# Output projection of a hybrid encoder block: eight pairs of token tiles with seven part products, placed in the up/down stream, in place of sixteen single tiles

## The chip, the cores and the metric

One core of one Trainium2 chip runs the whole program. The time is the device time of one execution in microseconds. The kernel before took 2931.34 us, the median of three runs (2931.17 to 2938.84).

## The reference, cut to what matters

The block has 2048 tokens of 1024 columns. An input projection feeds two groups of heads, a chunked mLSTM (y_A, 512 columns) and latent attention (y_B, 512 columns). Then:

```python
h = h + jnp.concatenate([y_a, y_b], axis=-1) @ w_out[l]          # 1024 x 1024
h = h + conv_gated_mlp(rms_norm(h, ln_ffn_g[l]), w_up[l], ...)   # d_ff 2816, 2 x 2816 columns up
gate = jax.nn.sigmoid(rms_norm(h, ple_norm_g[l]) @ w_ple_gate[l])
h = h + gate * rms_norm(p[l] @ w_ple_proj[l], ple_post_g[l])
out = rms_norm(h, final_g)
```

The change concerns the first of these lines and the normalisation that opens the second.

## The kernel before

Every matrix product is made to the accuracy of fp32 from three products of high and low parts: `split` (L108) writes a copy rounded to fp32r on ACT (L119) and the rest by a subtraction on DVE (L122), and `mm3` (L129) issues low x high, high x low and high x high (L132). A token tile is 128 tokens; there are 16.

`run` (L149) calls the stages in order: the input projection, `attend`, `out_proj`, `up_down`. Each has its own tiles in SBUF, named by tags ("w5", "x10", "u1", "t0"); a new tile on a tag waits until the last reader of the old one is done. PSUM has eight banks: while attention and output projection run, four of them are "sc" (`bank`), two "tr" (`tbank`), one "pv" and one "ml". After `out_proj` these pools are closed and others are opened for the up stage, two of [x, y] and two of [z, spare].

**Attention** (`attend`, L1193) runs 64 rounds, one for each of 4 heads x 16 token tiles. The order of a round is written out by hand (L1232): score banks of the next tile ("s0" to "s3"), their exponentials ("E", "e"), transposes ("t"), the product with the values ("V"), and a dot for each place at which the mLSTM, which runs beside it as a generator, may take a step. `SIDE` (617) sets how many steps are spread over the 64 rounds; what is left of it is done after the last round. The row sums of the softmax are collected, inverted, transposed and stored to `ri_d` in two halves (`sums`, L1244), through a tile "ri" on the tag u1.

**Output projection** (`out_proj`, L1349). The 1024 rows of the weights are eight k-tiles. Their splits stay in SBUF ("wo"); those of the mLSTM half are scaled by that group's gain. `load_y(c)` (L1327) loads the turned columns of a token tile ("yr") and the reciprocal row sums, spread over all partitions ("rb", through `row_bcast`, L145), multiplies the attention half by them (L1332) and splits ("yhl"). Then come, for both column halves, 8 k-tiles x 3 products into a bank, and DVE adds the bank to the tile of x (L1383). The rows go to `h1_d` (L1384), for the residual later. `norm_load` (L1297) squares and sums the row on ACT, makes the inverse root on POOL, and scales the row by it and by the gain g2 in place with one operation of DVE (L1303), which must wait for the store to `h1_d`. One tile later eight transposes of TensorE turn it (L1312), ACT copies the two banks (L1313), and the turned tile goes to `x2_d`. In between lie loads of the convolution taps and the operands of the first block of the up stage: `sums(0)` reads four 128x512 pieces of `x2_d` back at a time, makes four sums on DVE, splits three of the operands (B11, T1, T2) and stores the other two to `t_d`.

**Up and down stage** (`up_down`, L1649). It goes by blocks and, within a block, by pairs. A pair is a product of a 2 x 2 array of parts A (stationary operand, split by `up_prep`) with a 2 x 2 array B (moving operand, 512 columns, split by `load_op` or `sum4`), made with seven part products in place of eight:

```
T1 = B12 - B11   T2 = B22 - T1   T3 = T2 - B11   T4 = B21 - T2
S1 = A21 + A22   S2 = S1 - A11   S3 = A11 - A21  S4 = A12 - S2
A11 B11,  S1 T1,  S2 T2,  A12 B21,  S3 T3,  A22 T4,  S4 B22
```

Each part product is 4 k-tiles x 3 products of 512 columns (`prod`, L507; the products at L512). A22 T4 and S4 B22 of a pair are issued in the middle of the next one (`rest_y`, L1664; `rest_z`, L1679), and with them what is added to them. The loop (`for i in range(n)`) has seven places at which other work is let in (`side(1)` to `side(7)`), and at a block's end the operands of the next are loaded there. Pairs 0 and 1 are written a little differently from the others, since the operands of block 0 are only then complete.

Of the kernel before, what the change touches and what calls it, by code (L numbers as in the profile page):

```python
# [37 lines left out]
SIDE = 617  # L38
# [22 lines left out]
class Block:  # L61
# [4 lines left out]
    def __init__(self, ctx, tc, d):  # L66
# [31 lines left out]
        self.t_d = dt([2, 4, P, 4, 512], F32, name="t_d")  # L98
        self.tw_d = dt([4, 4, P, 4, 512], F32, name="tw_d")
# [49 lines left out]
    def run(self, out):  # L149
# [9 lines left out]
        self.attend(tail(self.mlstm()))  # L159
        self.out_proj()  # L160
        right.close()
        pools(right, "right", ("fa", 2))
        left.close()
        pools(left, "left", ("fb", 2))
        self.up_down(out)
# [16 lines left out]
    def in_proj(self):  # L182
# [158 lines left out]
        cols = self.cst.tile([P, 8], F32, name="cols")  # L341
# [851 lines left out]
    def attend(self, side):  # L1193
# [50 lines left out]
        def sums(half):  # L1244

            pt = self.tbank([NH * 8, P])
            nc.tensor.transpose(pt, rsums[:, half * NH * 8:(half + 1) * NH * 8], self.ident)
# [4 lines left out]
        cur, self.wo = self.first, []  # L1252
        pts, pend = [], None
        for i, (h, qt) in enumerate(seq):
            if h == NH - 1 and qt in (4, 6, 8, 10):
                self.load_wo(qt // 2 - 2)
            if h == NH - 1 and qt == 9:
                sums(0)
            if i == len(seq) - 2:
                self.y0 = self.load_y(0)  # L1260
# [5 lines left out]
            if nxt is None:  # L1266
                self.ps0 = self.pml.tile([P, 512], F32, name="wo0", tag="ml")
                self.out_mm(self.ps0, self.y0, range(4), slice(0, 512))
            for op in order:
                if op == ".":  # L1270
                    pump()
                elif op[0] == "s" and nxt:
                    score_bank(nxt, int(op[1]))
                elif op[0] == "t":
# [15 lines left out]
            cur = nxt  # L1290
        pv(pend, 1)
        sums(1)
        for _ in side:
            pass


    def norm_load(self, h, g, ssq_junk):  # L1297

        nc = self.nc
        ssq = self.stat(1, "nt_s")  # L1300
        nc.scalar.activation(ssq_junk, h, AF.Square, accum_out=ssq)
        r = self.rsq(ssq, 1, 1.0 / D)
        nc.vector.scalar_tensor_tensor(h, h, r, g, op0=ALU.mult, op1=ALU.mult)  # L1303

    def transpose_out(self, xn, otag, dst):
        nc = self.nc
        pt = (self.tbank(), self.tbank())
        xo = self.at(otag, [P, KT, P], name="nt_o")
        for f in range(2):
            for j in range(4):  # L1310
                kt = f * 4 + j
                nc.tensor.transpose(pt[f][:, j, :], xn[:, kt * P:(kt + 1) * P], self.ident)  # L1312
            nc.scalar.copy(xo[:, f * 4:f * 4 + 4], pt[f])  # L1313
        nc.sync.dma_start(dst, xo)

    def load_wo(self, k):
        nc = self.nc
        raw = self.at(("w13", "w13", "w13", "w13", "w13", "w12", "u2", "w0")[k], [P, D], name="wor")
        nc.sync.dma_start(raw, self.d["w_out"][0, k * P:(k + 1) * P, :] if k < 4 else self.wo_d[k - 4])
        w = self.at(f"x{(0, 1, 2, 3, 6, 7, 4, 5)[k]}", [P, 2, D], F32R, f"wo{k}")  # L1320
        if k < NH:
            self.split_g(raw, self.gmix[:, k:k + 1], w[:, 0], w[:, 1])
        else:
            self.split(raw, w[:, 0], w[:, 1])
        self.wo.append(w)

    def load_y(self, c):  # L1327
        yr = self.at(f"w{5 + c % 2}", [P, 8, P], name="yr")
        self.nc.sync.dma_start(yr, self.y_d[c])
# [83 lines left out]

# [754 lines left out]
```

## Time and profile before

| | |
|---|---|
| median of three runs | 2931.34 us |
| the profiled execution | 2930.37 us, span 2928.6 us, mean granted clock 0.994 |
| input projection and start (0 to 200 us) | PE busy 182.59 us |
| attention (200 to 1160) | PE busy 948.84, DVE 721.19, ACT 548.61 |
| end of attention (1160 to 1228) | PE busy 60.44 of 68.00 |
| output projection and first operands (1228 to 1420) | PE busy 188.55 of 192.00, DVE 97.13, ACT 63.70 |
| up stage (1420 to 2160) | PE busy 737.31 of 740.00 |
| down stage, gate and end (2160 to 2930) | PE busy 742.80 of 770.00 |

The profile comes from one execution. Times are microseconds; a group's row has its busy time, the mean of one instruction in ns, and the idle time of the engine just before it with what ended that. PE is TensorE, DVE VectorE, ACT ScalarE, POOL GpSimd, and SP issues nearly all DMAs, in one queue. A timeline's row has start, busy time, engine, line, operation, and in brackets the wait before it and what ended the wait.

### The profile page before, as it was taken

How to read it: one execution, taken by the hardware profiler on the slowest of the kernel's cores; microseconds unless marked ns; L12 is line 12 of the kernel's file. 1: busy time of each engine (PE TensorE's matmuls, PEld its weight loads, DVE VectorE, ACT ScalarE, POOL GpSimd, SP SyncE). 2: the span in 40 equal slices, each digit the busy share in tenths (PEclk: the TensorE clock that was granted, in tenths of full speed). 3: DMA queues.
4: the chain of work that ended last, by engine and by line, in shares of the span. 5: the costliest groups of instructions: out<-in, count | busy, mean ns of one | idle time of the engine just before them, and what ended most of it. 6: DMA issues, size and time to landing. Idle time of an engine off the chain costs nothing.

```text
span 2928.6 us, 40726 instructions
## 1 busy us (share of the span) xinstructions
PE 2860.5 (98%) x14543; PEld 2405.6 (82%) x14543; DVE 2098.0 (72%) x3727; ACT 1525.7 (52%) x2919; POOL 152.6 (5%) x295
## 2 busy tenths in 40 slices
PE   8899999999999999899999999999999999999998
PEld 7788888988988898788788887888887788888776
DVE  7566878767777777535777777777778766676776
ACT  7544556555666665423555555655556333244664
POOL 4100000000000000000000000000000000002011
PEclk9999999999999999999999999999999999999999
DMA  9766655443333343468635544657776657575864
GB/s 276 219 197 183 185 169 167 136 128 96 96 101 106 105 128 104 140 202 282 207 132 189 178 170 158 193 181 236 233 237 201 225 200 230 179 245 202 284 190 151
DMA packets 424954, 530.19 MB, mean 181 GB/s; under 512 B 31504, under 2 KB 286512, under 8 KB 424752
## 3 DMA queue, kind: packets, MB, share of 16 engines
q1 hardware_dynamic: 424752, 527.60, 56.2%
q8 instruction: 114, 1.87, 0.3%
q14 instruction: 88, 0.72, 0.1%
HBM read 347.49 MB, written 180.02 MB: 180 GB/s over the span
## 4 chain that ended last, share of the span: by engine, by line
PE 78%; DVE 7%; DMA 6%; ACT 4%; issue 3%; POOL 1%; SPq 0%; POOLq 0%; ACTq 0%; DVEq 0%
PE fxy L512 30%; PE fz L512 12%; PE bk L132 7%; PE ppv L132 5%; PE bk L512 4%; PE tb L1209 3%; PE tb L512 2%; PE bk L1146 2%; PE bk L1148 2%; PE bk L1150 2%; PE bk L1147 2%; PE bk L1149 2%; PE fs L132 1%; PE mb L1085 1%; PE mb L1086 1%
## 5 line engine op out<-in xcount | busy, mean ns | idle before, releaser
L512 PE MATMUL fxy<-op,fw 128*128 128x512 f32 x3552 | 856.1, 393 | 15.9 <-DVE fh L1653 4.6
L512 PEld LDWEIGHTS fxy<-op,fw 128*128 128x128 f32 x3552 | 662.0, 188 | 174.2 <-ACT ug L1817 12.9
L512 PE MATMUL fz<-op,fw 128*128 128x512 f32 x1776 | 441.2, 391 | 5.4 <-DVE xt L1383 2.6
L512 PEld LDWEIGHTS fz<-op,fw 128*128 128x128 f32 x1776 | 332.8, 188 | 74.9 <-DVE xt L1383 2.8
L119 ACT CAST pt<-tb 128x512 fp32r<-128x512 f32 x256 | 147.3, 586 | 188.1 <-PE tb L1209 187.3
L512 PE MATMUL fxy<-op,fwd 128*128 128x512 f32 (+1 forms) x888 | 214.0, 389 | 1.0 <-ACT gate L2001 0.8
L1151 DVE TENSOR_REDUCE mx<-bk 128x1 f32<-128x512 f32 x255 | 174.7, 685 | 47.0 <-PE bk L1150 46.4
L132 PE MATMUL ppv<-pt,kv 128*128 128x256 f32 x1536 | 204.9, 288 | 0.0
L122 DVE TENSOR_TENSOR pt<-tb,pt 128x512 fp32r<-128x512 f32 x256 | 174.4, 686 | 31.0 <-ACT pt L119 29.9
L512 PEld LDWEIGHTS fxy<-op,fwd 128*128 128x128 f32 x888 | 165.1, 188 | 36.0 <-ACT gate L2001 1.2
L132 PEld LDWEIGHTS ppv<-pt,kv 128*128 128x128 f32 x1536 | 190.1, 192 | 0.3 <-ACT pt L119 0.3
L1169 ACT ACTIVATE pe<-bk,nm 128x512 f32<-128x512 f32 x255 | 173.8, 696 | 27.4 <-DVE nm L1163 26.3
L132 PE MATMUL bk<-wo,yhl 128*128 128x512 f32 x744 | 176.4, 395 | 5.8 <-DVE yhl L122 5.8
L132 PEld LDWEIGHTS bk<-wo,yhl 128*128 128x128 f32 x744 | 139.5, 190 | 34.8 <-DVE yhl L122 6.2
L132 PE MATMUL bk<-wsp,xh 128*128 128x464 f32 (+1 forms) x512 | 156.5, 387 | 0.0
L1209 PE MATMUL tb<-ident,pe 128*128 128x128 f32 x1024 | 149.8, 273 | 4.0 <-DVE pt L122 3.6
L1209 PEld LDWEIGHTS tb<-ident,pe 128*128 128x128 f32 x1024 | 121.6, 140 | 23.1 <-DVE pt L122 7.0
L119 ACT CAST fw<-hraw 128x1024 fp32r<-128x1024 f32 (+1 forms) x72 | 70.2, 981 | 125.2 <-PE fxy L512 96.0
L1653 DVE TENSOR_TENSOR fh<-fh,fxy 128x512 f32<-128x512 f32 x95 | 65.1, 686 | 91.8 <-PE fxy L512 91.3
L122 DVE TENSOR_TENSOR fw<-fwr,fw 128x1024 fp32r<-128x1024 f32 x88 | 107.5, 1221 | 29.2 <-ACT fw L119 29.2
L1704 DVE SCALAR_TENSOR_TENSOR fgv<-uv,fcw,fgv 128x1024 f32<-128x1024 f32 x88 | 112.8, 1282 | 10.6 <-ACT fgv L1702 9.9
L1146 PE MATMUL bk<-kv,q_s 128*128 128x512 f32 x255 | 114.4, 449 | 1.0 <-ACT pe L1169 1.0
(431 smaller groups left out, 5025.8 us busy)
## 6 DMA issues: line engine op xcount, KB each, us to landing
fwr<-in_w_up SPq DMA_DIRECT2D x66, 512.0 KB, 4.7
fh<-h_d SPq DMA_DIRECT2D x48, 512.0 KB, 3.7
h_d<-fh SPq DMA_DIRECT2D x48, 512.0 KB, 4.5
s_d<-fwr SPq DMA_DIRECT2D x44, 512.0 KB, 2.6
fws<-s_d SPq DMA_DIRECT2D x44, 512.0 KB, 3.9
rw<-row_d SPq DMA_DIRECT2D x32, 512.0 KB, 5.0
tw_d<-tsum SPq DMA_DIRECT2D x60, 256.0 KB, 5.4
opr<-tw_d SPq DMA_DIRECT2D x60, 256.0 KB, 4.6
```

What stands on the lines that cost most here:

```text
L119: nc.scalar.copy(hi, src)
L122: (sub or nc.vector).tensor_tensor(lo, src, _f(hi), op=ALU.subtract)
L132: mm = lambda *a, **k: self.nc.tensor.matmul(*a, **k, skip_group_check=more)
L512: self.nc.tensor.matmul(out, a[:, k * P:(k + 1) * P], parts[lo][:, cols], start=first, stop=lo == 1 and k == last, skip_group_check=more)
L1146: mm(ps, ql, kh[:, ks], start=True, stop=False)
L1147: mm(ps, qr, self.krl[:, ks], start=False, stop=False)
L1148: mm(ps, qh, kl[:, ks], start=False, stop=False)
L1151: nc.vector.tensor_reduce(s.mx[:, kb:kb + 1], ps, axis=AX.X, op=ALU.max)
L1169: nc.scalar.activation(s.pe[:, kb % 2], s.banks[kb], AF.Exp, bias=s.nm, scale=ASCALE, accum_out=s.rs[:, kb:kb + 1])
L1209: nc.tensor.transpose(t[:, j, :], s.p[kb][:, j * P:(j + 1) * P], self.ident)
L1653: add = lambda o, a, b: tt(o, a, b, op=ALU.add)
L1704: nc.vector.scalar_tensor_tensor(t, u[:, tap:tap + 2 * SB], taps[:, tap, ct:ct + 1], t, op0=ALU.mult, op1=ALU.add)
```

## The change

**The projection becomes eight pairs.** `out_proj`, `load_wo`, `load_y`, `out_mm`, `norm_load` and `transpose_out` are gone. `up_down` becomes a generator `stream`, whose loop starts at pair -8. In pairs -8 to -1, A is two token tiles (rows) by two halves of the 1024 columns of y, and B is `w_out` as 2 x 2 parts of 512 x 512. Pairs -8 to -5 hold the tiles c and c + 4 (c = 0 to 3), pairs -4 to -1 the tiles 8, 9 to 14, 15.

**The operands of the weights.** `out_sums` makes T1 to T4 of the weights in rounds 33 to 60 of attention and stores them to `two_d`; the splits of B11 and T1 follow there. T2, B21 and T3 are loaded and split in the last rounds, T4 and B22 right after the last.

**The end of attention.** The mLSTM's steps are spread with `SIDE` 660 and all done four rounds before the end. The first pair's tiles are loaded then. In the last round, which has no scores, the generator issues A11 B11 and S1 T1 of pair -8 at "s0" and "s2". "ri" lies on the tag s2 in place of u1.

**The rows.** The norm is in `norm`: squares in two halves on ACT, the sum and the inverse root on POOL, and the scaling in place by ACT, behind the store to `h1_d`. The gain g2 is applied later: `turn` makes four transposes into a bank and four scaled copies of 128 columns each on ACT. The first row of a pair is turned two pairs later at places 2 and 3 (`old`), the second one pair later at 6 and 7 (`prev`).

**Sums of block 0 on chip.** `sums4` makes T1 to T4 of block 0 from the turned tiles c and c + 4 while they are in SBUF and stores them to `t_d`. The turned tile of the half B12 is not stored in these pairs. Block 0 is then loaded like every other block, while pair -1 runs, and pairs 0 and 1 are written like the others. PSUM keeps the pools of attention to the end: x and y from "sc", z from "tr", the spare bank from "pv" and "ml" in turn. The places of the split operands in SBUF (OPX, PAIRS) are dealt anew.

The diff, cut to its core:

```diff
-SIDE = 617
+SIDE = 660
-        self.attend(tail(self.mlstm()))
-        self.out_proj()
...
-        self.up_down(out)
+        self.attend(tail(self.mlstm()), self.stream(out))
...
-            o = self.at("u1", [NH * 8, P], name="ri")
+            o = self.at("s2", [NH * 8, P], name="ri")
...
+        last = {"s0": lambda: next(stream), "s2": lambda: next(stream), "s3": lambda: self.op_split("T3")}
+            if 33 <= i < 61:
+                next(wout, None)
+            if i == n - 4:
+                for _ in side:
+                    pass
+                self.up_load(-8)
+                self.op_load("T2", ("t0", "t1", "t2", "t3"))
+            if i == n - 3:
+                later = self.up_prep(-8)
+            if i == n - 2:
+                self.op_load("B21", ("t4", "t5", "u0"))
+            if i == n - 1:
+                self.op_split("T2")
+                later()
+                self.op_load("T3", ("u1", "t0", "t1"))
+                self.op_split("B21")
...
+        self.op_load("T4", ("t2", "t3", "t4", "t5"))
+        self.up_load(-7)
         pv(pend, 1)
         sums(1)
+        self.op_split("T4")
+        self.op_load("B22", ("t0", "t1", "t2", "t3"))
+        self.op_split("B22")
...
+        for e, tag in enumerate(("w12", "w13", "w0", "w1")[i % 2 * 2:i % 2 * 2 + 2]):
+            c = self.out_tile(i, e)
+            t = self.at(tag, [P, 8, P], name="yr")
+            self.nc.sync.dma_start(t, self.y_d[c])
+            raw[i].append((t, self.row_bcast(self.at(f"t{6 + e}", [P, SB], name="rb"), self.ri_d[c].rearrange("h t -> (h t)"), SB)))
...
+        def norm(s, e):
+            h, ssq, half = s.o[e], self.stat(2, "nts"), self.stat(1, "nt_s")
+            nc.sync.dma_start(self.h1_d[self.out_tile(s.i, e)], h)
+            for f, fs in enumerate((L, H)):
+                nc.scalar.activation(self.at("s2", [P, SB], BF16, "junk"), h[:, fs], AF.Square, accum_out=ssq[:, f:f + 1])
+            nc.gpsimd.tensor_tensor(half, ssq[:, 0:1], ssq[:, 1:2], op=ALU.add)
+            r = self.rsq(half, 1, 1.0 / D)
+            nc.scalar.activation(h, h, AF.Copy, scale=r)
+        def turn(s, e, f, bank):
+            pt = bank.rearrange("p (k t) -> p k t", t=P)
+            for j in range(4):
+                nc.tensor.transpose(pt[:, j, :], s.o[e][:, (f * 4 + j) * P:(f * 4 + j + 1) * P], self.ident)
+            xo = self.at(f"t{f if s.i < -4 and not e else 4 + f}", [P, 4, P], name="nt_o")
+            for j in range(4):
+                nc.scalar.activation(xo[:, j], pt[:, j], AF.Copy, scale=self.g2[:, f * 4 + j:f * 4 + j + 1])
...
+        def begin(at):
+            bank = prev.spare if at % 2 and prev and prev.spare is not None else s.spare
+            if at in (6, 7) and prev and prev.out:
+                turn(prev, 1, at - 6, bank)
+            if at in (2, 3) and old and old.out:
+                turn(old, 0, at - 2, bank)
+            if at in (3, 4, 5) and old and old.i < -4:
+                sums4(old, at)
...
-        for i in range(n):
+        for i in range(-8, n):
```

In the order of TensorE, the end of attention before. The last products of the first token tile are mixed with the last transposes of the mLSTM (mb<-ident,hy); "wo" numbered 12186 to 13287 are k-tiles of the weights, and the first row with wo_11630 opens token tile 1.

```order
L1113 MATMUL mb<-ident,hy 128x128 x4
L132 MATMUL bk<-wo_12186,yhl 128x512
L132 MATMUL bk<-wo_12478,yhl 128x512 x3
L132 MATMUL bk<-wo_13272,yhl 128x512 x3
L132 MATMUL bk<-wo_13277,yhl 128x512 x3
L132 MATMUL bk<-wo_13282,yhl 128x512 x3
L132 MATMUL bk<-wo_13287,yhl 128x512 x3
L132 MATMUL bk<-wo_11630,yhl 128x512 x3
L132 MATMUL bk<-wo_11889,yhl 128x512 x3
```

The same place after: behind the last products with the values (ppv) and the transpose of the row sums (tb<-ident,gt). fw_13270 and 13271 hold S2 and S4 of pair -8, fw_13043 and 13044 its A11 and A12, fw_13052 its S3 and S1; fw_13485 is A11 of pair -7.

```order
L133 MATMUL ppv<-pt,kv_4664 128x256 x2
L1242 MATMUL tb<-ident,gt 32x128
L507 MATMUL bk<-op,fw_13270 128x512 x3
L507 MATMUL bk<-op,fw_13271 128x512 x4
L507 MATMUL bk<-op,fw_13270 128x512 x4
L507 MATMUL bk<-op,fw_13043 128x512 x4
L507 MATMUL bk<-op,fw_13044 128x512 x4
L507 MATMUL bk<-op,fw_13043 128x512 x4
L507 MATMUL bk<-op,fw_13485 128x512 x3
L507 MATMUL bk<-op,fw_13052 128x512 x4
```

The mLSTM's transposes have moved ahead of this place, and between the last product with the values and the first operand of pair -7 stand 23 products of pair -8.

In SP's queue, the same place before: the last store of attention's output (y_d<-ya), the second half of the row sums (ri_d<-ri), the weights of the first up pair (fwr), then the loads of token tile 1.

```order
L1227 DMA y_d<-ya 128x128 x2
L1250 DMA ri_d<-ri 32x128
L1562 DMA fwr<-in_w_up 128x8x128
L1329 DMA yr<-y_d 128x1024
L1115 DMA y_d<-hy 128x512
L146 DMA rb<-ri_d 128x512
L1354 DMA xt<-in_x 128x1024
L1384 DMA h_d<-xt 128x1024
L146 DMA rb<-ri_d 128x512 x2
```

After: opw are pieces of the output weights (here B22), yr and rb the tiles and row sums of the pairs.

```order
L1575 DMA xt<-in_x 128x1024
L1566 DMA yr<-y_d 128x1024 x3
L1362 DMA opw<-wo_d 128x512 x4
L1222 DMA y_d<-ya 128x128 x2
L1245 DMA ri_d<-ri 32x128
L147 DMA rb<-ri_d 128x512 x2
L1575 DMA xt<-in_x 128x1024
```

The loads of the tiles and of B22 now stand ahead of the last store of attention's output, and no store of the mLSTM stands between them and their row sums.

On ACT in the projection, before, while the operands of block 0 are made: casts of the token tiles (yhl) and of block 0's operands (op<-tsum), the squares (junk), the copies of the turned tile (nt_o).

```order
L119 CAST yhl<-yr 128x1024
L119 CAST op<-tsum 128x512
L1313 COPY nt_o<-tb 128x512 x2
L1301 ACTIVATE junk,nt_s<-xt 128x1024
L119 CAST op<-tsum 128x512 x3
```

After, in pair -4: the squares of both rows in halves (L1697), the scaling (L1700), the casts of the next pair's operands (fw), and the scaled copies of 128 columns (L1710).

```order
L1697 ACTIVATE junk,nts<-xt 128x512
L1710 ACTIVATE nt_o<-fs,cols 128x128
L1697 ACTIVATE junk,nts<-xt 128x512 x2
L1700 ACTIVATE xt<-xt,rsr 128x1024
L120 CAST fw_14246<-yr 128x1024
L120 CAST fw_14240<-yr 128x1024
L1710 ACTIVATE nt_o<-fs,cols 128x128
L1697 ACTIVATE junk,nts<-xt 128x512
L1710 ACTIVATE nt_o<-fs,cols 128x128 x3
L120 CAST fw_14434<-yr 128x1024
L1710 ACTIVATE nt_o<-fs,cols 128x128 x4
L1700 ACTIVATE xt<-xt,rsr 128x1024
```

The scaling of the whole row, and 16 small copies for each pair, are new on ACT; the next pair's casts stand behind the scaling.

More of the change, by code (lines that the diff above doesn't have):

```diff
@@ L1273, in attend @@
                     score_bank(nxt, int(op[1]))
+                elif op in last and not nxt:
+                    last[op]()
                 elif op[0] == "t":
@@ L1316, in load_wo @@
[L1316 to L1325, printed above, removed]
```

366 lines of the change are left out of this document (182 added, 184 removed).

## The prediction

> **What bounds the kernel now.** I read the page first, then the stretches of time with the busy time of each engine, then TensorE's timeline around the stage that is changed, and last the chain of waits there.
>
> ```profile
> span 2928.6 us, 40726 instructions
> PE 2860.5 (98%) x14543; PEld 2405.6 (82%) x14543; DVE 2098.0 (72%) x3727; ACT 1525.7 (52%) x2919; POOL 152.6 (5%) x295
> ```
>
> TensorE is busy for 98% of the span, and no other engine is near that. A microsecond is won only by giving TensorE fewer products or by closing one of its few gaps. The next rows show where the gaps of the changed stretch are (the columns are the length of the stretch, busy us of PE, its weight loads, DVE, ACT and POOL, the granted clock, the DMA share and GB/s).
>
> ```profile
> 1220.00:1240.00 20.00, 14.20 (x54) 11.26 (x54) 5.97 (x7) 2.19 (x3) 0.77 (x2) 0.83 0.58 180
> 1246.00:1340.00 94.00, 94.00 (x447) 77.56 (x446) 37.62 (x49) 24.60 (x41) 5.10 (x14) 1.00 0.61 205
> 1340.00:1380.00 40.00, 39.84 (x188) 33.01 (x187) 28.46 (x41) 16.34 (x28) 2.94 (x8) 1.00 0.93 306
> 1400.00:1420.00 20.00, 17.43 (x75) 13.95 (x73) 13.34 (x18) 11.87 (x23) 1.69 (x4) 0.91 0.94 294
> 1420.00:1790.00 370.00, 370.00 (x1630) 303.51 (x1630) 282.66 (x350) 193.48 (x269) 0.00 (x0) 1.00 0.48 165
> ```
>
> Inside the output projection (1246 to 1380) TensorE has no gap, and DVE and ACT are at 40% and 26%. The gaps are at its two ends. The up stage that follows runs 370 us without a gap, with DVE at 76%. TensorE's timeline gives the ends and the pace:
>
> ```profile
> 1205.49 0.51 PE L132 MATMUL wo<-wo,yhl 128*128 128x512 f32 x1 [0.70 <-ACT wo L119]
> 1208.52 5.76 PE L132 MATMUL ppv<-pt,kv 128*128 128x256 f32 x46
> 1214.12 0.27 PE L1247 MATMUL tb<-ident,gt 128*32 128x128 f32 x1
> 1215.40 0.50 PE L132 MATMUL wo<-wo,yhl 128*128 128x512 f32 x1 [0.31 <-ACT wo L119]
> 1216.66 0.74 PE L132 MATMUL wo<-wo,yhl 128*128 128x512 f32 x2 [0.76 <-DVE wo L122]
> 1228.31 13.03 PE L132 MATMUL bk<-wo,yhl 128*128 128x512 f32 x48 [5.80 <-DVE yhl L122]
> 1384.89 1.06 PE L1312 MATMUL tb<-ident,xt 128*128 128x128 f32 x8 [0.41 <-DVE xt L1303]
> 1397.52 11.14 PE L132 MATMUL bk<-wo,yhl 128*128 128x512 f32 x48
> 1412.11 4.20 PE L512 MATMUL fz<-op,fw 128*128 128x512 f32 x11 [2.57 <-DVE xt L1383]
> 1416.10 3.13 PE L512 MATMUL fxy<-op,fw 128*128 128x512 f32 x12
> ...
> 1450.57 2.88 PE L512 MATMUL fz<-op,fw 128*128 128x512 f32 x12
> 1453.29 2.88 PE L512 MATMUL fxy<-op,fwd 128*128 128x512 f32 x12
> ```
>
> The pace is 2.72 us for 12 products of 512 columns (1450.57 to 1453.29), 0.2267 us each. A product of PV takes 5.60 / 46 = 0.122 us. The waits in brackets are 0.70 + 0.31 + 0.76 + 5.80 + 0.41 + 2.57 = 10.55 us. After the two long ones the granted clock is 0.83 and 0.91: the 48 products at 1228.31 take 13.03 us where 48 at 1397.52 take 11.14 (1.9 lost), and the 11 at 1412.11 take 3.99 us to the next start instead of 11 x 0.2267 = 2.49 (1.5 lost). Together 13.95 us.
>
> What the 5.80 us wait for is in the chain of waits, in order of time:
>
> ```profile
> 1219.95 0.25 SPq L1115
> ...
> 1220.30 4.90 DMA rb<-ri_d
> ...
> 1225.22 0.70 DVE yr L1332
> ...
> 1225.95 1.05 ACT yhl L119
> ```
>
> Token tile 1 waits for its row of reciprocal sums (rb), whose load is issued only at 1220.30, behind a store of the mLSTM side work (L1115) in SP's queue.
>
> **The change, part by part.** The sum is made against the profiled execution's own 2930.37 us; the median of the runs is 2931.34, so 0.97 is added at the end.
>
> *Fewer products.* Before: 16 tiles x 2 column halves x 8 k-tiles x 3 (high and low parts) = 768. After: 8 pairs x 7 part products x 4 k-tiles x 3 = 672. 96 x 0.2267 = **-21.8 us**. All are on the path, since TensorE has no gap there. The 128 transposes of the token tiles stay.
>
> *The gaps of before go:* **-13.95 us**, to be replaced by what is late next.
>
> The old clock dip follows a gap of 2.57 us as well as one of 5.80. The Trainium skill, page "TensorE: Matmul & The Clock Gate", Part 1, lets the clock fall only after an idle window of about 3.4 us. By that rule the 2.57 us would have cost no clock and this term would be 12.45; the trace shows otherwise, and I keep its 1.5.
>
> *The last three rounds with scores.* The side work now ends four rounds before the end (SIDE 660 instead of 617), and its place is taken by the preparation of the first pair. These rounds hold 60 score products (13.6 us), 48 transposes and 72 PV products (8.8).
>
> ```profile
> L1151 DVE TENSOR_REDUCE mx<-bk 128x1 f32<-128x512 f32 x255 | 174.7, 685 | 47.0 <-PE bk L1150 46.4
> L122 DVE TENSOR_TENSOR fw<-fwr,fw 128x1024 fp32r<-128x1024 f32 x88 | 107.5, 1221 | 29.2 <-ACT fw L119 29.2
> L119 ACT CAST fw<-fwr 128x1024 fp32r<-128x1024 f32 x88 | 92.5, 1053 | 26.2 <-PE fxy L512 15.1 <-DVE fwr L1642 4.1 <-PE fz L512 4.1
> L1642 DVE TENSOR_TENSOR fwr<-fwr 128x512 f32<-128x512 f32 x22 | 15.2, 692 | 0.5
> L1312 PE MATMUL tb<-ident,xt 128*128 128x128 f32 x120 | 15.6, 273 | 0.6 <-DVE xt L1303 0.6
> ```
>
> Eight transposes take 0.82 us of TensorE (1384.89 to about 1385.71 by their row), so 48 take some 4.9, and TensorE has 27.3 us of work. DVE has 12 maxima and 12 halves of the split of pt at 0.69 (16.4), seven operations of 0.692 and two of 1.221 of the preparation (7.3), two weight splits (1.4) and small ones (about 2): 27.1. DVE is as full as TensorE there, and TensorE waits for DVE's maxima. I take **+1.0**; ends 0 and 3.
>
> *The last round.* TensorE gets 24 products of the first pair (before: 22) beside 6 groups of transposes and 72 PV products, 16.5 us. ACT is the longer chain: 4 exponentials with their sums (0.91 each), one cast of 1.05, the copies of two banks, nine casts of weights at 0.62 (T2's last, B21, T3) ahead of the last cast of pt, 13.5 us, which can start only some 2.6 us after the last score. The last PV product then ends near 19 us: **+2.5**; ends 1 and 4.
>
> *The second pair's tiles.* They go into the buffers of the last exponentials, so their loads wait for the last transposes, about 4.5 us before the last PV product ends. Loads of 512 KB landed in 4.0 us at the median (below); then follow 0.69, 1.05 and 1.22. TensorE has 23 products (5.2 us) of the first pair meanwhile, so the first product of the second pair starts about in time. But DVE then has 9 more operations (splits of B22, four adds and sums) ahead of the split that S1 needs: I get 1.1 and 1.3 us of wait, **+2.4**; ends 0 and 6. Behind the loads SP holds B22, which has 21 us.
>
> *The eight pairs.* TensorE: 84 products and 16 transposes, 20.5 us. DVE: 3 splits at 1.22 and one at 0.69, two row scalings, four sums, six adds into the rows and (first four pairs) four sums of the turned tiles: 15.3 us. ACT, from these rows:
>
> ```profile
> L1095 ACT ACTIVATE hy<-mb,den 128x128 f32<-128x128 f32 x64 | 20.2, 371 | 14.1 <-DVE den L1091 10.5 <-PE mb L1086 2.2 <-PE bk L1149 1.4
> L1313 ACT COPY nt_o<-tb 128x512 f32<-128x512 f32 x30 | 15.9, 578 | 0.0
> L2020 ACT ACTIVATE junk<-hb 128x512 bf16<-128x512 f32 x31 | 19.5, 628 | 18.5 <-DVE hb L2007 18.5
> L1303 DVE SCALAR_TENSOR_TENSOR xt<-xt,rsr,g 128x1024 f32<-128x1024 f32 x16 | 20.5, 1283 | 21.6 <-DMA h_d<-xt 21.6
> ```
>
> Casts 3.8, copy 0.6, four squares with their read-out 3.3, two scalings of 1024 columns 2.1, and 16 scaled copies of 128 columns at 0.371 = 5.9: 15.7 us of 20.5. Before, four copies of 512 did that last part in 2.3. The Trainium skill, "VectorE: DVE Perf Modes", section on the TRN2 errata, says against this cut that ScalarE pays a fixed cost per instruction, 172 cycles of 1.2 GHz from PSUM; by its table 16 small ones are an estimated 4.0 us and ACT's sum 13.8. Row and rule agree that small copies are dear; the row is dearer, and I use the row.
>
> Nothing fills its 20.5 us, so the pairs should run at TensorE's pace. The added wait is the in-place scaling of the rows on ACT: it waits for the store of the same rows, as DVE did at L1303 (21.6 us over 16 tiles, 1.35 each). Queued behind it on ACT are the next pair's casts and the scaled copies that free the banks. From the last add to the transposes there are 36 products (8.2 us); the add, the longer of store (3.1) and squares with POOL, and the scaling need about 6. I take 0.45 us for each pair, **+3.5**; ends 0 and 12.
>
> *Entry into the up stage.* Weights of block 0 are now loaded and split while the last pair runs, as block 1's are at 1810 to 1830:
>
> ```profile
> 1826.10 4.61 PE L512 MATMUL fxy<-op,fw 128*128 128x512 f32 x12 [2.69 <-ACT ug L1817]
> 1830.54 1.53 PE L512 MATMUL fz<-op,fw 128*128 128x512 f32 x6
> ```
>
> There TensorE waited 2.69 us, and 12 products took 4.44 instead of 2.72: **+4.4**; ends 2.7 and 8. The up stage itself is not touched beyond other PSUM banks: nothing.
>
> Sum: -21.8 - 13.95 + 1.0 + 2.5 + 2.4 + 3.5 + 4.4 = -21.95. 2930.37 - 21.95 + 0.97 = **2909 us**. With the low ends (3.7 new) it is 2899, with most of the high ends (26 of 33) 2922.
>
> **The rivals.**
>
> *The scaling's wait falls on TensorE in full* (ACT's queue is strict in order, and 36 products are little cover): 16 x 1.35 = 21.6 instead of 3.5, **2927**, no change that can be told. For it: L1303's row. Against it: the store is issued while the squares run. Chance 0.10.
>
> *The second pair's tiles come late* (the loads share the DMA engines with T4 and B22, 2 MB): each microsecond is one of TensorE, some 7 more, and the clock dips: **2917**. Against it: the load of tile 1 landed in 4.90 us at 0.6 DMA share. Chance 0.09.
>
> *The DMA engines become the bound.*
>
> ```profile
> yr<-y_d SPq DMA_DIRECT2D x16, 512.0 KB, 4.0
> xt<-in_x SPq DMA_DIRECT2D x16, 512.0 KB, 5.6
> h_d<-xt SPq DMA_DIRECT2D x16, 512.0 KB, 3.1
> x_d<-nt_o SPq DMA_DIRECT2D x16, 512.0 KB, 4.9
> rb<-ri_d SPq DMA_DIRECT2D x16, 256.0 KB, 3.4
> ```
>
> A pair moves 2 x (512 + 512 + 512 + 256) KB, 768 KB of turned tiles and 1024 KB of their sums: 5.5 MB (4.7 in the last four), 268 GB/s at 20.5 us. If the queue gave only the 205 GB/s of the old projection, a pair would take 26.9 (23.0) us: 35.6 instead of 3.5, **2941**, slower. It decides from about 217 GB/s down, where nothing is left of the gain. Against it: 205 GB/s came at a share of 0.61, and 306 were moved from 1340 to 1380 at 0.93. Chance 0.04.
>
> That the change does not do what it says is excluded by the count of products.
>
> **How the numbers follow.** Forecast 0.77 at 2909, then 0.10, 0.09, 0.04. A measurement can tell about 0.3%, 8.8 us: faster means below 2922.5, slower above 2940.1. Faster: 0.77 less 0.02 for its upper tail, 0.09, and 0.02 of the first rival: 0.86. Same: 0.10. Slower: 0.04. The range reaches from the low ends with 3 us for a stage that I cost at nothing, 2896, to the edge of the first rival, 2926.
>
> **What would show it.** Right: 672 products where 768 were, no wait over 3 us after the last PV product, eight pairs 20.5 to 21.5 us apart, ACT near 77% and DVE near 75% there, DMA near 260 GB/s. Wrong: pairs 22 us or more apart, with the transposes waiting for the scaling (first rival) or for no engine but DMA (third); a wait of over 5 us ahead of the second pair; or an up stage whose gaps grew.

## The result, and the profile after

The kernel after takes 2894.42 us (median of four runs, 2889.63 to 2895.95); the kernel before, run beside it, 2931.26. The ratio is 0.9868, 95% interval 0.9846 to 0.9891. The forecast was 2909 us with a range down to 2896: the direction was right, the gain was 36.8 us where 22 were forecast, and the time lies 1.6 us below the range. The profiled execution took 2894.34 us.

```profile
span 2892.3 us, 40961 instructions
PE 2827.0 (98%) x14447; PEld 2388.7 (83%) x14447; DVE 2134.6 (74%) x3802; ACT 1590.9 (55%) x3116; POOL 162.2 (6%) x311
```

TensorE has lost 33.5 us of busy time (2860.5 before), and is still the bound at 98%.

To see where the 36.3 us of the two spans came from, both programs are cut at points where the same work begins: the transpose of attention's row sums (tb<-ident,gt) and A11 B11 of the third up pair. The first rows are before (the gt transpose at 1214.12, the third pair at 1447.85), the second after (1217.64 and 1423.74). Columns as in the prediction.

```profile
1214.12:1447.85 233.73, 223.73 (x1030) 182.95 (x1027) 123.23 (x161) 81.22 (x130) 12.47 (x32) 0.98 0.69 227
1447.85:2928.59 1480.74, 1452.26 (x6405) 1184.44 (x6403) 1086.84 (x1436) 745.08 (x1152) 49.04 (x113) 1.00 0.61 200
```

```profile
1217.64:1423.74 206.10, 197.82 (x926) 160.49 (x924) 141.88 (x201) 136.26 (x301) 20.85 (x48) 1.00 0.81 254
1423.74:2892.26 1468.52, 1444.12 (x6405) 1190.45 (x6403) 1084.42 (x1432) 744.95 (x1154) 50.40 (x113) 1.00 0.62 202
```

Up to the row sums after is 3.5 us later; the changed stretch is 27.6 us shorter; together 24.1, beside a forecast of 21.95. The other **12.2 us** come after the third up pair, with the same 6405 products in both. The prediction had this stretch at nothing.

In the changed stretch the prediction's marks are met in part. TensorE's timeline has these waits of over 1 us:

```profile
1224.92 5.07 PE L507 MATMUL bk<-op,fw 128*128 128x512 f32 x21 [1.09 <-DVE xt L1647]
1341.02 0.66 PE L1707 MATMUL fs<-ident,xt 128*128 128x128 f32 x4 [1.12 <-ACT xt L1700]
1376.30 0.66 PE L1707 MATMUL fs<-ident,xt 128*128 128x128 f32 x4 [2.30 <-ACT xt L1700]
1409.12 0.66 PE L1707 MATMUL fs<-ident,xt 128*128 128x128 f32 x4 [1.44 <-ACT xt L1700]
```

The 5.80 us wait ahead of the second tile is gone; 1.09 us stand ahead of the second pair. Pairs -6 to -2 take 21.3 to 22.3 us, pair -1, beside which block 0 is loaded, 23.5 (1356.44 to 1379.93):

```profile
1247.99:1269.39 21.40, 21.18 (x104) 17.26 (x102) 14.21 (x20) 12.32 (x29) 1.46 (x3) 1.00 0.81 248
1356.44:1379.93 23.49, 21.19 (x104) 17.27 (x102) 16.02 (x25) 18.23 (x40) 1.84 (x4) 1.00 0.89 286
```

ScalarE is at 78% in pair -1 and at 58% in pair -6, VectorE at 68% and 66%; the DMA engines move 286 and 248 GB/s. The transposes do wait for the scaling, as the prediction's sign for its first rival has it, but for 7.1 us in all and not for 21.6.

Now the stretch behind. Before, in an up pair of block 0 (TensorE first, then ScalarE; fxy is the tile of x and y, fz holds z):

```profile
1450.57 2.88 PE L512 MATMUL fz<-op,fw 128*128 128x512 f32 x12
...
1458.73 1.07 PE L512 MATMUL fz<-op,fw 128*128 128x512 f32 x4
1459.63 2.98 PE L512 MATMUL fxy<-op,fw 128*128 128x512 f32 x12
1462.45 1.98 PE L512 MATMUL fz<-op,fw 128*128 128x512 f32 x8
...
1469.71 2.88 PE L512 MATMUL fz<-op,fw 128*128 128x512 f32 x12
```

```profile
1458.98 0.59 ACT L1817 COPY ug<-fxy 128x512 f32<-128x512 f32 x1 [0.81 <-PE fxy L512]
```

After, the same pair:

```profile
1426.46 2.88 PE L507 MATMUL tb<-op,fw 128*128 128x512 f32 x12
1429.18 2.88 PE L507 MATMUL bk<-op,fwd 128*128 128x512 f32 x12
1431.90 5.60 PE L507 MATMUL bk<-op,fw 128*128 128x512 f32 x24
1437.34 2.88 PE L507 MATMUL tb<-op,fw 128*128 128x512 f32 x12
...
1445.50 2.88 PE L507 MATMUL tb<-op,fw 128*128 128x512 f32 x12
```

Before, S4 B22 (1458.73, fz), which stands behind A12 B21 in the program, was begun ahead of it and broken after four products, and A12 B21 (1459.63, fxy) began when ScalarE's copy of y (1458.98 + 0.59 = 1459.57) was done, although it writes x. The 12 products then took 2.82 us to the next start instead of 2.72, and the pair 19.14 us (1450.57 to 1469.71). x and y were two halves of one tile, and the wait is for the tile. After, each has a tile of its own: S2 T2 and A12 B21 run as 24 products in a row, and the pair takes 19.04. In the second block it is 19.21 (2010.63 to 2029.84) beside the same 19.04. A tenth or two of a microsecond is small, but there are some 60 such pairs (an estimate of 6 to 10 us), and in the list of TensorE's waits behind the third pair the same wait has larger cases. Before, then after (us in total, times, longest):

```profile
PE fxy L512 <- DVE fh L1653: 4.8, 5, 2.2
PE fxy L512 <- ACT ug L1817: 4.2, 2, 2.7
PE fxy L512 <- ACT c L1811: 4.0, 5, 1.6
PE fxy L512 <- DVE p L1653: 3.1, 1, 3.1
```

```profile
PE bk L507 <- DVE fh L1647: 4.0, 2, 2.4
PE tb L507 <- DVE ug L1647: 3.9, 3, 2.2
PE tb L507 <- ACT fw L120: 3.0, 3, 1.2
PE bk L507 <- DVE fw L123: 2.1, 1, 2.1
```

ug L1817 and c L1811 are copies of y; they are gone from the list after. The full lists add up to 19.7 and 14.5 us, so the listed waits hold 5.2 of the 12.2 us, and the small loss in each pair covers the rest.

### The profile page after: what moved, and what is told of

Read it like the earlier page. It is cut to its first block, busy times and chain, and to the rows that moved or that the text cites. A ratio compares the mean times of both kernels' runs of the same rounds, so it can differ in the third digit from the quotient of the medians.

```text
span 2892.3 us, 40961 instructions
## 1 busy us (share of the span) xinstructions
PE 2827.0 (98%) x14447; PEld 2388.7 (83%) x14447; DVE 2134.6 (74%) x3802; ACT 1590.9 (55%) x3116; POOL 162.2 (6%) x311
## 4 chain that ended last, share of the span: by engine, by line
PE 77%; DMA 8%; DVE 7%; ACT 4%; issue 2%; POOL 1%; SPq 0%; POOLq 0%; ACTq 0%; DVEq 0%
PE bk L507 35%; PE tb L507 14%; PE ppv L133 5%; PE bk L133 4%; PE tb L1204 3%; PE bk L1141 2%; PE bk L1145 2%; PE bk L1143 2%; PE bk L1144 2%; PE bk L1142 2%; PE fs L133 1%; DMA h_d<-xt 1%; DMA opr<-t_d 1%; DVE op L123 1%; PE mb L1080 1%
## 5 line engine op out<-in xcount | busy, mean ns | idle before, releaser
L507 PE MATMUL bk<-op,fw 128*128 128x512 f32 x4344 | 1026.0, 391 | 3.4 <-DVE fw L123 2.1
L507 PEld LDWEIGHTS bk<-op,fw 128*128 128x128 f32 x4344 | 813.5, 188 | 172.6 <-DVE fw L123 2.5
L507 PE MATMUL tb<-op,fw 128*128 128x512 f32 x2160 | 524.7, 391 | 10.2 <-DVE ug L1647 3.9
L507 PEld LDWEIGHTS tb<-op,fw 128*128 128x128 f32 x2160 | 404.2, 188 | 98.2 <-ACT fw L120 8.2
L507 PE MATMUL bk<-op,fwd 128*128 128x512 f32 (+1 forms) x1128 | 274.5, 391 | 4.5 <-DVE fh L1647 4.0
L507 PEld LDWEIGHTS bk<-op,fwd 128*128 128x128 f32 x1128 | 210.2, 188 | 49.3 <-DVE fh L1647 4.9
L1146 DVE TENSOR_REDUCE mx<-bk 128x1 f32<-128x512 f32 x255 | 174.3, 684 | 49.8 <-PE bk L1145 49.1
L1204 PEld LDWEIGHTS tb<-ident,pe 128*128 128x128 f32 x1024 | 121.6, 141 | 22.3 <-DVE pt L123 6.6
L120 ACT CAST op<-opr 128x512 fp32r<-128x512 f32 x165 | 97.6, 618 | 67.5 <-PE bk L507 18.4
L123 DVE TENSOR_TENSOR op<-opr,op 128x512 fp32r<-128x512 f32 x165 | 107.8, 686 | 33.3 <-ACT op L120 31.7
L1647 DVE TENSOR_TENSOR fh<-fh,bk 128x512 f32<-128x512 f32 x95 | 65.0, 684 | 74.9 <-PE bk L507 74.7
```

The source lines that it names most:

```text
L120: nc.scalar.copy(hi, src)
L123: (sub or nc.vector).tensor_tensor(lo, src, _f(hi), op=ALU.subtract)
L507: self.nc.tensor.matmul(out, a[:, k * P:(k + 1) * P], parts[lo][:, cols], start=first, stop=lo == 1 and k == last, skip_group_check=more)
L1146: nc.vector.tensor_reduce(s.mx[:, kb:kb + 1], ps, axis=AX.X, op=ALU.max)
L1204: nc.tensor.transpose(t[:, j, :], s.p[kb][:, j * P:(j + 1) * P], self.ident)
L1647: add = lambda o, a, b: tt(o, a, b, op=ALU.add)
```

## The experiments

Each was timed beside the kernel before (2930.3 to 2932.6 in these sessions). Five of them leave out or change a part of the result: rows not stored, S3 T3 left out (three kernels) or made twice.

| kernel | median us | ratio to before (95%) | row sums / third pair begins / rest of the span |
|---|---|---|---|
| before | 2931.3 | | 1214.1 / 1447.9 / 1480.7 |
| after | 2894.4 | 0.9868 (0.9846 to 0.9891) | 1217.6 / 1423.7 / 1468.5 |
| before, x and y apart | 2919.2 | 0.9955 (0.9938 to 0.9971) | 1209.7 / 1444.4 / 1467.7 |
| that, and row sums early | 2909.9 | 0.9925 (0.9909 to 0.9941) | 1210.7 / 1437.6 / 1466.3 |
| after, added reading of x | 2898.9 | 0.9886 (0.9871 to 0.9902) | 1215.8 / 1423.3 / 1468.3 |
| after, rows in halves | 2890.4 | 0.9864 (0.9846 to 0.9882) | 1215.8 / 1422.0 / 1467.2 |
| after, rows not stored | 2893.8 | 0.9870 (0.9853 to 0.9888) | 1216.8 / 1422.5 / 1468.0 |
| after, gain on VectorE | 2885.2 | 0.9838 (0.9824 to 0.9853) | 1216.6 / 1418.9 / 1464.3 |
| halves and gain on VectorE | 2885.5 | 0.9844 (0.9826 to 0.9861) | 1216.8 / 1417.8 / 1466.4 |
| after, without S3 T3 | 2878.9 | 0.9831 (0.9812 to 0.9851) | 1216.6 / 1407.7 / 1466.6 |
| halves, without S3 T3 | 2879.4 | 0.9814 (0.9794 to 0.9834) | 1214.6 / 1407.3 / 1470.5 |
| halves, gain, without S3 T3 | 2877.0 | 0.9809 (0.9793 to 0.9824) | 1216.4 / 1408.6 / 1467.5 |
| halves, gain, SIDE 617 | 2899.6 | 0.9886 (0.9870 to 0.9903) | 1224.5 / 1426.4 / 1467.8 |
| after, S3 T3 twice | 2912.3 | 0.9927 (0.9914 to 0.9940) | 1214.9 / 1440.3 / 1472.5 |

The last column is from each profiled execution: when the row sums are transposed, when the third up pair begins, and how long the rest takes. Kernels whose code is the same up to the row sums differ there by up to 4.4 us, so a change between the row sums and the third pair is read from the difference of the first two numbers.

### x and y apart in the kernel before

```diff
-            xy = self.pfa.tile([P, 2, SB], F32, name="fxy", tag="fxy")
-            x, s.y = xy[:, 0], xy[:, 1]
+            x, s.y = [self.pfa.tile([P, SB], F32, name=t, tag=t) for t in ("fx", "fy")]
```

> The kernel before, with one thing changed: x and y of a pair in the up and down stage are two tiles of one bank each, where they were two halves of one tile (the same eight banks of PSUM). The theory: 12.2 of the 36.3 us came after the third up pair, because the kernel after has x and y in banks of their own. In the kernel before, A12 B21, which writes x, waits for the engine that still reads y, as both are one tile: 0.10 to 0.17 us in each pair, and more where a block begins. By it this kernel takes 2919 to 2925 us (6 to 12 less than 2931), a pair of block 0 takes 19.04 us instead of 19.14, and A12 B21 has no wait ahead of it. The rival: the 12.2 us are what entries into stages and half-clock windows happen to cost in any new order of the instructions. By it this kernel stays within 2928 to 2934.

Measured: 2919.18 us, 12.2 less than the 2931.38 beside it. All six runs lie below all eleven of the kernel before in that session. In the profiled execution the rest of the span behind the third pair (the second row) fell by 13.0 us, to what it is after, and the stretch from the row sums to the third pair (the first row) stayed:

```profile
1209.68:1444.43 234.75, 223.31 (x1030) 183.23 (x1027) 123.02 (x161) 81.72 (x130) 12.69 (x32) 0.98 0.69 226
1444.43:2912.14 1467.71, 1443.53 (x6405) 1190.27 (x6403) 1086.59 (x1436) 745.41 (x1151) 49.63 (x113) 0.99 0.62 202
```

A pair of block 0 takes 19.04 us (1447.15 to 1466.19), with no break in S4 B22. The theory stands: the 12.2 us behind the third pair that the prediction missed are this edit, as far as the runs can tell (95% interval 8.5 to 18.2 us). All 13 kernels with x and y apart have 1464 to 1473 us behind the third pair; only the kernel before has 1481.

### The wait put back in the kernel after

```diff
                 nc.scalar.copy(s.ug[:, 2 + SB:2 + 2 * SB], s.y)
+                nc.scalar.copy(self.stat(1, "again"), x[:, 0:1])
...
                 add(s.o[0][:, H], s.o[0][:, H], s.y)
+                if s.down:
+                    nc.vector.tensor_copy(self.stat(1, "again"), x[:, 0:1])
```

> The kernel after, with the wait put back: behind the first reading of y (by ScalarE in the up pairs, by VectorE in the down pairs) stands a reading of one column of x on the same engine, so that A12 B21 must wait for it. By the theory (x and y in one tile cost 12.2 us) it takes 2900 to 2906 us, pairs take 19.15 to 19.3 us, and there are small waits ahead of A12 B21. By the rival (entries and clock windows of a new order) it stays within 2891 to 2897, as the added reading is 0.2 us on engines that have room.

Measured: 2898.90 us, outside both, and it decides nothing, since the wait did not come back in the regular pairs:

```profile
1426.74 0.17 ACT L1865 COPY again<-bk 128x1 f32<-128x1 f32 x1
...
1434.42 0.59 ACT L1864 COPY ug<-bk 128x512 f32<-128x512 f32 x1 [0.41 <-PE bk L507]
```

The added reading needs only x, so it was moved 7.7 us ahead of the copy of y, and S2 T2 and A12 B21 stayed 24 products in a row. TensorE did wait for the added reading in three places, once at the entry into block 0 and twice in the down stage, 4 us in all:

```profile
PE bk L507 <- DVE again L1856: 2.3, 2, 1.6
PE bk L507 <- ACT again L1865: 1.8, 1, 1.8
```

In the profiled execution (2894.29 us) the rest of the span stayed at 1468.3 us even so: the listed waits there add up to 17.1 us beside 14.5, but the clock was halved twice less. The other four executions took 2898.7 to 2899.9 us.

### The early row sums, in the kernel before

On top of x and y apart:

```diff
-            o = self.at("u1", [NH * 8, P], name="ri")
+            o = self.at("s2", [NH * 8, P], name="ri")
```

> The kernel before with x and y in tiles of their own and, in addition, the transposed row sums (ri) on the tag s2 as in the kernel after, so that the row sums of token tile 1 are loaded before the last rounds end. Theory: the 5.80 us wait and the clock lost behind it (1.9 us) were this one load. By it 5 to 8 us less than the kernel with x and y apart alone (2919), so 2911 to 2914 us, and no wait over 2 us ahead of token tile 1. Rival: token tile 1 is held by the next thing in the queue (its own columns or the last store of the mLSTM); then 2917 to 2920.

Measured: 2909.92 us, 9.3 less than with x and y apart alone, a little more than the theory had; between the two profiled executions the stretch from the row sums to the third pair is 7.9 us shorter (226.81 beside 234.75). Token tile 1 now follows tile 0 with no wait (x62, no bracket), where 5.80 us stood before:

```profile
1215.53 14.33 PE L132 MATMUL bk<-wo,yhl 128*128 128x512 f32 x62
...
1402.21 4.04 PE L512 MATMUL fz<-op,fw 128*128 128x512 f32 x11 [2.57 <-DVE xt L1383]
```

The wait ahead of the up stage remains. Two edits of a line or two thus give 21.4 of the 36.8 us with the sixteen single tiles kept; by difference, all the rest of the change brings 15.5.

### The rows' store: in halves, and left out

In halves, each half stored when its last sum is done:

```diff
+                if s.out:
+                    nc.sync.dma_start(self.h1_d[self.out_tile(i, 0)][:, L], s.o[0][:, L])
...
+                if s.out:
+                    nc.sync.dma_start(self.h1_d[self.out_tile(i, 1)][:, H], s.o[1][:, H])
...
-            nc.sync.dma_start(self.h1_d[self.out_tile(s.i, e)], h)
+            late = L if e else H
+            nc.sync.dma_start(self.h1_d[self.out_tile(s.i, e)][:, late], h[:, late])
```

> The kernel after, with the rows of the projection stored in two halves: the half that is complete first is stored as soon as it is complete, so that the scaling in place waits only for a store of 256 KB. The theory of the first rival of the prediction: the scaling (L1700) waits 33.5 us for the store of the same rows, and 7.1 us of that reach TensorE at the transposes. By it the kernel takes 2888 to 2892 us, and the waits of the transposes for L1700 fall from 7.1 to under 3 us. The rival: landing is set by what else the DMA engines move (0.8 to 0.9 busy there), not by the size of the store; then the time is 2892 to 2897 and the waits stay.

Left out (the down stage then adds to x in place of the rows; that line is not shown):

```diff
-            nc.sync.dma_start(self.h1_d[self.out_tile(s.i, e)], h)
```

> The kernel after without the store of the projection's rows; the down stage adds to x in place of them (this part of the result is left out). It prices the wait of the scaling for that store in full. If the store's wait is what lengthens the pairs: 2885 to 2889 us, and no wait of the transposes for L1700 above 0.5 us. If ScalarE's own queue does (squares, casts and small copies ahead of the scaling): 2889 to 2893, with 3 us or more of waits of the transposes left.

Measured: 2890.42 (2889.53 to 2896.73) and 2893.79 us. The first meets the theory's two signs, the time and the shorter wait, but neither can be told from 2894.42 (2889.63 to 2895.95), and the stretch from the row sums to the third pair is 206.2 and 205.7 us beside 206.1. In halves the waits for the scaling fell to 2.6 us, but 3.6 us for the small copies of the bank had come up beside them:

```profile
PE fs L1708 <- ACT nt_o L1711: 3.6, 3, 2.4
PE fs L1708 <- ACT xt L1701: 2.6, 2, 2.4
```

The run without any store settles it; its time lies just above the range for ScalarE's own queue, and 5 us above the end of the range for the store. The transposes' waits, from the row sums to 1425 us, are 7.1 us in the kernel after (first row), and 6.7 without the store:

```profile
PE fs L1707 <- ACT xt L1700: 7.1, 7, 2.3
```

```profile
PE fs L1706 <- ACT nt_o L1709: 6.7, 3, 3.2
```

The trace names the store as what ScalarE waits for (33.5 us at L1700), but without the store the same time is waited one step on, for the small copies that free the bank. The wait had moved, not gone.

### The gain on VectorE

```diff
-            for j in range(4):
-                nc.scalar.activation(xo[:, j], pt[:, j], AF.Copy, scale=self.g2[:, f * 4 + j:f * 4 + j + 1])
+            tt(xo, pt, self.g2[:, f * 4:f * 4 + 4].unsqueeze(2).broadcast_to([P, 4, P]), op=ALU.mult)
```

With rows in halves:

> The kernel after with the rows stored in halves, and the turned bank read by one multiplication of 512 columns on VectorE (the gain spread along the tokens) in place of four scaled copies of 128 on ScalarE: 128 small operations fewer on ScalarE, 32 of about 0.69 us more on VectorE. With halves the transposes still wait 3.6 us for these small copies and 2.6 us for the scaling. Theory (ScalarE's queue is what is left): 2885 to 2888 us. Rival (VectorE becomes late with the splits of block 0): 2890 to 2896.

Alone:

> The kernel after with one thing changed: the turned bank is read by one multiplication of 512 columns on VectorE (the gain spread along the tokens) in place of four scaled copies of 128 on ScalarE. Rows are stored whole. Without any store of the rows the time did not fall (2893.8), with store in halves and gain on VectorE it fell to 2885.5. Theory: what holds the transposes in the pairs is ScalarE's queue, in which the small copies stand; then this edit alone gives 6 to 9 us, 2885 to 2889, and the stage from the row sums to the third up pair takes about 231 us instead of 236. Rival: store in halves and gain on VectorE are both needed, since the scaling still waits for a whole store; then 2890 to 2894.

Measured: 2885.45 and 2885.23 us. The edit alone gives 9.2 us, and halves add nothing to it. It is the fastest kernel here that computes the whole result: all its runs (2885.1 to 2887.5) lie below all runs of the kernel after (from 2889.6). The transposes' waits for the scaling fell to 3.3 us (the first three rows), while ScalarE's scaling still waited 31.9 us for the store (the last):

```profile
PE fs L1707 <- ACT xt L1700: 3.3, 2, 1.8
PE bk L507 <- DVE xt L1647: 1.4, 1, 1.4
PE fs L1707 <- ACT bk L1823: 0.8, 1, 0.8
ACT xt L1700 <- DMA h_d<-xt: 31.9, 13, 3.8
```

Of the 9.2 us, 3.8 lie in the changed stretch (202.3 us from the row sums to the third pair, beside 206.1; the 236 and 231 of the expectation are not the length of this stage). 1.1 lie ahead of the row sums, where the edit changes nothing, and 4.2 behind the third pair. What makes those, no run tells; in the profiled executions the clock was halved once less there, and the listed waits are 2 us shorter. The edit takes away both the number of instructions and the load of ScalarE, and no run separates the two.

### The price of 96 products

Less, in three kernels, by leaving S3 T3 out of the eight pairs:

```diff
-            prod(s.y, s.ops["S3"], "T3", True)
+            if not s.out:
+                prod(s.y, s.ops["S3"], "T3", True)
```

> The kernel after without the part product S3 T3 in the eight pairs of the projection: 96 products fewer, as many as the change itself takes away. The theory that TensorE is what bounds the pairs: 17 to 22 us less (96 x 0.2267 = 21.8, less what the shorter cover adds to the waits), 2872 to 2878. The rival, that ScalarE or the DMA engines bound them (0.8 to 0.9 of the DMA engines busy, ScalarE at 0.6): less than 8 us, 2887 to 2895, with longer waits of the transposes.

> The kernel after with the rows stored in halves, and without the part product S3 T3 in the eight pairs (left out, 96 products fewer). Leaving it out gave 15.5 us where 21.8 us of products went, beside rows stored whole. Theory: the difference is the scaling's wait for the store, which the shorter pairs no longer hide; with halves 18 to 22 us come off 2890.4, so 2868 to 2872. Rival: what is short is room on ScalarE; then 12 to 16 us come off, 2874 to 2878.

> The kernel with rows stored in halves and the gain on VectorE, and without the part product S3 T3 in the eight pairs (left out, 96 products fewer). Beside the small copies on ScalarE those 96 products were worth 15.5 us (rows whole) and 11.0 us (rows in halves), not 21.8. Theory: ScalarE's queue took the rest; with it shorter 17 to 21 us come off 2885.5, so 2864 to 2869. Rival: a pair of 17.7 us is too short for any order of the row's chain of add, squares, scaling and transposes; then 10 to 15 us come off, 2870 to 2876.

More, by making it twice in the kernel after:

> The kernel after with the part product S3 T3 made twice in each of the eight pairs of the projection (added twice, so that part of the result is changed): 96 products more, as many as the eighth part product would be. Theory: in the direction of the change a product costs TensorE's pace, since the pairs with seven still have TensorE as their bound for all but some 7 us of waits; by it 15 to 22 us more than 2894.4, 2909 to 2916. Rival: ScalarE's queue sets the length of a pair (leaving S3 T3 out gave only 15.5, and 8.5 with the shorter queue); by it less than 8 us more, under 2902.

Measured: 15.5 us less, 11.0 less, 8.5 less, and 17.9 more. The first lies between the two theories, the second and the third below even their rivals, so none of the explanations gave the size. All three end at 2877 to 2879 us. Their pairs seem to have another bound, on which the halves and the gain no longer tell; which one was not tested. Upward, where the change was made, the price is near TensorE's (21.8): 17.9 us by the medians, and 19.3 in the profiled execution between the row sums and the third pair. Part of the difference is the transposes' wait for the scaling, which falls from 7.1 to 4.5 us:

```profile
PE fs L1707 <- ACT xt L1700: 4.5, 3, 3.7
```

### The mLSTM's steps as before

```diff
-SIDE = 660
+SIDE = 617
```

> The kernel with rows stored in halves and the gain on VectorE, with the mLSTM's steps spread as before (SIDE 617 instead of 660), what is left of them being done in one go four rounds before the end. From the start of attention to the row sums the kernel after takes 1005 to 1007 us in its profiled runs, the kernel before 999 to 1004. Theory: the denser spread with the weight sums costs 2 to 4 us of small waits of the scores and transposes; with 617 these fall, and 2882 to 2885 is reached. Rival: the steps left over, done in one go, cost TensorE as much or more there: 2885 to 2892.

Measured: 2899.60 us, 14.2 more than the same kernel with 660 (9.3 between the two profiled executions). The theory falls, and the rival was too mild. The transpose of the row sums comes at 1224.47 with 617 and at 1216.78 with 660:

```profile
1224.47 0.27 PE L1242 MATMUL tb<-ident,gt 128*32 128x128 f32 x1
```

```profile
1216.78 0.27 PE L1242 MATMUL tb<-ident,gt 128*32 128x128 f32 x1
```

In front of its last four rounds (the 240th of 256 splits of pt on VectorE) the kernel with 617 is 12 us earlier, 1161.4 beside 1173.8; it then needs 63.0 us for them instead of 43.0, since the left-over steps come one behind the other, with TensorE waiting and its granted clock at 0.92 there, beside 1.00:

```profile
PE bk L1141 <- ACT pe L1164: 3.9, 1, 3.9
PE mb L1108 <- DVE hy L1104: 3.6, 1, 3.6
```

## Why the forecast was wrong

*The step that failed* is the end of the entry's paragraph: "The up stage itself is not touched beyond other PSUM banks: nothing." The banks were the point: x and y got tiles of their own, and 12.2 us came off behind the third pair, 12.2 by the run that makes this edit alone. The quoted row at 1826.10 even named it: A12 B21, which writes x, had waited 2.69 us for ug L1817, a copy of y. I took that wait as the price of a block's beginning, and did not ask why a product into x should wait for a reader of y. Without the banks the change is worth 24.6 us (36.8 less 12.2), beside 22 forecast; the direction was right. But that this sum is near is in part luck, as two of its terms have the right size from other causes.

*Fewer products, -21.8:* right as a mechanism, with 17.9 us measured for 96 products in that direction. The 20.5 us for TensorE's work in a pair were too few: by the rates given it is 20.7, and the trace has 21.2 (21.40 less a wait of 0.22 in pair -6). No term of the sum was made from it.

*The waits of before, -13.95:* taking the wait ahead of tile 1 away alone gave 9.3 us, of which the trace of before has 7.7 (5.80 and 1.9 of clock). The wait of 2.57 us ahead of the up stage went too.

*Rounds with scores and last round, +3.5:* the row sums come 3.5 us later in the two profiled executions, but not by what those rounds take; that the size agrees is luck. From the 240th split of pt on they take 43.0 us beside 49.1 before, 6.1 less and not 3.5 more. Up to there the kernel after takes 9.6 us more (1174.6 beside 1165.0); the steps of the mLSTM and the weight sums now stand there, and the sum has no term for them. The parts listed for ScalarE in the last round also add up to 11.4 us and not to 13.5; the casts of pt are not among them.

*Second pair's tiles, +2.4:* 1.09.

*Eight pairs and entry, +7.9:* 7.1 us of waits of the transposes by the list. The size was right by luck. The wait of A12 B21 at the entry into block 0 did not come at all, and in the pairs I named the scaling's wait for the store, as did the first rival. Leaving the store out gives nothing, taking the small copies off ScalarE gives 9.2, of which 3.8 in this stretch. My own sum for ScalarE had 5.9 us of small copies in a pair, and I took an engine at 77% as having room. The Trainium skill, "VectorE: DVE Perf Modes", section on the TRN2 errata, advises tiles of at least 512 elements against a latency of SBUF that each instruction pays once. In the trace of the kernel after the cost is seen with PSUM as the source: 0.367 us for a scaled copy of 128 columns and 0.583 for ScalarE's copy of 512, so four small ones take 1.47 us.

*The rivals:* the DMA engines moved 254 GB/s over the changed stretch, and no wait of TensorE there is put down to a DMA. The scaling's wait in full (21.6 us) did not come; its row (7.1 us) was there.

The Trainium skill, "PSUM — Partial Sum Buffer", section "Summary: rules for kernel authors", tells to read one bank while TensorE writes another, with semaphores by bank. By that rule x and y need no wait for each other, as they are two banks. The run with x and y apart agrees: without it, 12.2 us less.

## What to carry to other kernels

Where TensorE, writing one half of a tile, waits for an engine that reads the other half, the wait comes from how the tile was declared; look for it in the list of waits before costing a stage at nothing. The engine that a wait names is not yet its price: take the named cause away, and see whether the wait moves one step on. When a change alters how operands or banks are declared, every stage that uses them has to be costed, not only the one that was rewritten.

## What the runs showed of the hardware

The clock was halved for one or a few steps of 3.41 us at a time, but not after every long wait. In the kernel after, a wait of 2.30 us (up to 1376.30) was followed by full clock, and one of 2.09 us (up to 2750.79) by half. The last columns are the granted clock, the DMA share and GB/s:

```profile
1374.00:1376.30 2.30, 0.00 (x1) 0.00 (x0) 1.75 (x3) 1.20 (x2) 0.00 (x0) 1.00 0.86 223
1376.30:1379.70 3.40, 3.40 (x18) 2.83 (x19) 2.48 (x4) 3.29 (x5) 0.00 (x0) 1.00 1.02 404
2748.70:2750.80 2.10, 0.01 (x1) 0.01 (x1) 2.10 (x4) 0.72 (x2) 0.00 (x0) 1.00 0.98 339
2751.30:2754.70 3.40, 3.40 (x11) 2.54 (x10) 3.40 (x7) 2.26 (x3) 0.00 (x0) 0.50 0.95 293
```

In the kernel with rows in halves even 3.1 us cost no clock:

```profile
2247.30:2250.40 3.10, 0.02 (x1) 0.02 (x1) 1.99 (x5) 1.64 (x3) 0.00 (x0) 1.00 0.61 227
2250.40:2253.80 3.40, 3.40 (x15) 2.83 (x16) 3.40 (x5) 3.40 (x6) 0.00 (x0) 1.00 0.47 134
```

In the trace's clock record of the kernel before, the half-clock stretches begin at 1225.43, 1413.16 and 1826.17 us, 55 and 121 steps of 3.413 us apart, so they lie on a fixed grid. The Trainium skill, "TensorE: Matmul & The Clock Gate", Part 1, speaks of such a free-running window, and of one idle window of about 3.4 us that drops the clock. The grid agrees. The size does not: 2.09 us within one step were enough. What counts is how much of one step is idle: the 2.30 and 3.1 us that cost nothing lay across two steps (1.73 + 0.57 and 1.82 + 1.30). Counted by such steps over the 14 traces of this case, from 200 us on and without the last 15, each of the 38 steps in which TensorE was idle for 1.96 us or more was followed by half clock, 7 of the 36 with 1.59 to 1.95 us, and no drop began after one with less. A drop of one step costs up to 1.7 us (half of 3.41), by chance of where a wait falls; that may be part of why runs of one kernel differ by several us, which was not tested.
